# Sums that run on in PSUM: seven-product pairs of a hybrid attention block, and a 16-key tail in one product

## The chip, the cores and the metric

The kernel runs on one core of one Trainium2 chip. The metric is the device time of one execution in microseconds (us), the median of several runs. Before the change it is 909.74 us (three runs, 909.62 to 910.92). Engines are named as in the profile: PE (TensorE, matrix products), DVE (VectorE), ACT (ScalarE), POOL (GpSimd) and SP (SyncE, which here only issues loads).

## The reference

One encoder layer over 16 meta tokens and 1024 tokens of width 1024, everything in float32:

```python
hn = rmsnorm(h, pre_norm_g)
proj = hn @ w_in + b_in          # 1024 -> 5376 columns: q, k, v, z of two branches, gates ga and gb
oa = diff_attention(qa, ka, va)  # dense, 4 heads, two softmaxes each
ob = windowed_gqa(qb, kb, vb)    # each query sees keys within 128, 8 heads on 2 key heads
ya = (oa * silu(za)) @ w_out_a
yb = (ob * silu(zb)) @ w_out_b
mixed = sigmoid(ga) * ya + sigmoid(gb) * yb
h = h + rmsnorm(mixed @ w_out, post_norm_g)
return h[:, 16:]
```

## The kernel before

A float32 operand is held as the sum of a rounded part and a rest ("hi" and "lo", both in the fp32r format that PE multiplies fast), and a product of two operands is three products of parts. ACT (or POOL) rounds, DVE or POOL subtracts: line 791 and 792 in `split`, lines 139 and 140 in `load_w`.

The program is a chain of stages: normalization and transposition of the input, branch B's windowed attention, branch A's dense attention, the gates, the two output projections ("mix"), and the final product with w_out.

**Branch B** goes over four head pairs c and eight query blocks i. `b_trans` transposes the probabilities of a block, `b_values` multiplies them with the values. Block 0 sees two blocks of 128 keys and the 16 meta tokens, and takes the meta tokens as a third block: one matmul with the rounded probabilities and one with their rests.

**The gates** ga and gb (columns 3328 to 5375) and the final product are computed in pairs of 128-column blocks. A pair is one two-by-two block product, and instead of eight block products it takes seven, with sums of operands and of results (Strassen's scheme in Winograd's form). Each of the seven products P1 to P7 is twelve matmuls of 128x512 (line 862) into a PSUM tile of its own (`product`, six tiles). The operands of P1 and P2 and P4 on the weight side are plain; P5, P6, P3 and P7 need weight sums (`total`, line 837, into three "ws" buffers). On the input side P1, P2 and P3 are plain; P4 to P7 need sums of four quarters of the normalized input, which `combos` makes in nine pieces f1, f2, f4, f3 (lines 805 to 823, two pieces each, and a split at the end). Results are combined by DVE, one addition per step (line 871), or copied by ACT (line 869). The results are c11, c12, c21 and c22; a table gives the order of the products and what is added after each. `SEVEN` serves most pairs, `FIRST` the first output pair, `LAST` the last gate pair:

```python
SEVEN = (
    ("P1", (("p1", "P1"),)),
    ("P2", (("c11", "p1", "P2"),)),
    ("P6", (("u2", "p1", "P6"),)),
    ("P5", (("u4", "u2", "P5"),)),
    ("P3", (("c12", "u4", "P3"),)),
    ("P7", (("u3", "u2", "P7"), ("c22", "u3", "P5"))),
    ("P4", (("c21", "u3", "P4"),)))
```

Each ("name", sources) is one ACT copy (one source) or one DVE addition (two). A gate's result goes through a sigmoid (line 766) and, when both halves of a 128-row block are there, ACT stores it (`sg_d`, line 934). An output's result is squared with a row sum (ACT, line 1049), multiplied by the norm's weight (DVE, line 1051), and when a block of 128 rows is complete its inverse norm is computed (`rstd`) and the block is scaled and added to x in two halves (line 1070) and stored.

**Around the first gate pair.** Four products for branch A's z (`gate_a`, lines 884 and 885) run first; in each, the evacuation of the first half calls two pieces of `combos`, so eight pieces are made there and the ninth ahead of P6 of the first gate pair. After each of the four ga pairs `gate_b` loads branch B's z and o, applies silu and multiplies (lines 895 and 896). All these 128x1024 blocks live in the nine slots of one tile TB, handed out in rotation by `tl()`: call n gets slot n modulo 9, and its first writer waits for the last reader of call n - 9.

**What sets the order.** The code names operations in program order, and a scheduler places each on its engine's queue by the time it expects it to be ready; on the chip each engine then goes through its queue in that order. SP issues loads in its own order, and a load whose slot is not free holds up those behind it.

Of the kernel before, what the change touches and what calls it, by code (L numbers as in the profile page):

```python
# [78 lines left out]
def _body(ctx, tc, A, out, dbg, stop):  # L79
# [113 lines left out]
    VBM = sbp.tile([MT, 2, P], F32R, tag="am", name="vbm", bufs=1)  # L193
# [97 lines left out]

    def zeros(*x):
        z = sbp.tile([P, 256], F32, tag="sq", name="zero", bufs=1)[:80]
        pool.memset(z, 0.0)
        for y in x:
            pool.tensor_scalar(y, z[:, :y.shape[1]], 1.0, 1.0, ALU.mult, ALU.mult)
# [75 lines left out]
    def put_b(VB):  # L372
        def put(pt, b0, nb, rows):
            for g in range(2):
                src = pt[:, :, 64 * g:64 * g + 64]
                v = VB[g][:, b0:b0 + nb] if b0 < 8 else VBM[:, g:g + 1]
                hi = v[:, :, :64]
                act.activation(hi, src, AF.Copy)
                dve.tensor_tensor(v[:, :, 64:], src, hi, ALU.subtract)
        return put  # L380
# [39 lines left out]
    def b_trans(i, sb):  # L420
        ah = sbp.tile([P, 4, 256], F32R, tag="ah", name="ah")
        al = sbp.tile([P, 4, 256], F32R, tag="al", name="al")
        if i == 0:
            blocks = ((17, P, 0), (17 + P, P, 1), (1, MT, 8))
        else:
            blocks = tuple((1 + P * j, P, i - 1 + j) for j in range(3 if i < NB - 1 else 2))
        for x in range(0, len(blocks), 2):
            pt = psT.tile([P, 2, 256], F32, tag="pT", name="pT")
            sub = blocks[x:x + 2]
            for y, (o, rows, _) in enumerate(sub):  # L430
                for j in range(2):
                    pe.transpose(out=pt[:rows, y, j * P:(j + 1) * P], in_=sb[:, j, o:o + rows], identity=ident)  # L432
            rows, n = sub[0][1], len(sub)
            act.activation(ah[:rows, x:x + n], pt[:rows, :n], AF.Copy)
            dve.tensor_tensor(al[:rows, x:x + n], pt[:rows, :n], ah[:rows, x:x + n], ALU.subtract)
        return ah, al, blocks

    def b_values(i, ah, al, blocks, g, ob):
        VB = VB_[g]
        pv = psV.tile([P, 512], F32, tag="pv", name="pv")  # L440
        n, last = 0, 2 * len(blocks) - 1
        for a in (ah, al):
            for x, (_, rows, blk) in enumerate(blocks):
# [237 lines left out]
    am = sbp.tile([80, 256], F32R, tag="am", name="am", bufs=1)  # L681
    zeros(am)
# [28 lines left out]
    if stop == "A":  # L711
# [9 lines left out]
    SEVEN = (  # L721
        ("P1", (("p1", "P1"),)),
        ("P2", (("c11", "p1", "P2"),)),
        ("P6", (("u2", "p1", "P6"),)),
        ("P5", (("u4", "u2", "P5"),)),
        ("P3", (("c12", "u4", "P3"),)),
        ("P7", (("u3", "u2", "P7"), ("c22", "u3", "P5"))),
        ("P4", (("c21", "u3", "P4"),)))

    FIRST = (  # L730
        ("P1", (("p1", "P1"),)),
        ("P2", (("c11", "p1", "P2"),)),
        ("P3", ()),
        ("P6", (("u2", "p1", "P6"),)),
        ("P5", (("u4", "u2", "P5"), ("c12", "u4", "P3"))),
        ("P7", (("u3", "u2", "P7"), ("c22", "u3", "P5"))),
        ("P4", (("c21", "u3", "P4"),)))

    LAST = (
        ("P4", ()),  # L740
        ("P6", (("p6", "P6"),)),
        ("P5", (("u4", "p6", "P5"),)),
        ("P7", (("u3", "p6", "P7"), ("u5", "u3", "P5"), ("u6", "u3", "P4"))),
        ("P1", (("p1", "P1"), ("c22", "u5", "P1"), ("c21", "u6", "P1"), ("u7", "u4", "P1"))),
        ("P3", (("c12", "u7", "P3"),)),
        ("P2", (("c11", "p1", "P2"),)))
# [84 lines left out]
    def seven(steps, a, b, room, wroom, result, tmp=None, between={}, cut=None):  # L831

        val = dict(P1=a["a11"], P2=a["a12"], P4=a["a22"])

        def total(n, x, y, op):
            val[n] = wroom.tile([P, 4, P], F32, tag="ws", name="ws", bufs=3)
            dve.tensor_tensor(val[n], x, y, op)  # L837

        def operand(n):
            if n in ("P5", "P6", "P3") and "P5" not in val:  # L840
                total("P5", a["a21"], a["a22"], add)
            if n in ("P6", "P3") and "P6" not in val:
                total("P6", val["P5"], a["a11"], sub)
            if n == "P3":
                total(n, a["a12"], val["P6"], sub)
            if n == "P7":
                total(n, a["a11"], a["a21"], sub)
# [5 lines left out]
        x = {}  # L853
        for n, ops in steps:
            run(between.get(n, ()))
            hi, lo = operand(n)
            for cs in (slice(0, H),) if n != cut else (slice(0, H // 2), slice(H // 2, H)):
                x[n] = product()
                i = 0
                for w, part in ((hi, 0), (hi, 1), (lo, 0)):  # L860
                    for k in range(4):
                        pe.matmul(x[n][:, cs], lhsT=w[:, k], rhs=b[n][part][:, k, cs], start=(i == 0), stop=(i == 11))  # L862
                        i += 1
                for o, *src in ops:
                    if cs.start == 0:
                        x[o] = (tmp and tmp(o)) or room.tile([P, H], F32, tag="c", name="c", bufs=4 if tmp else 6)
                    src = [x[y][:, cs] for y in src]
                    if len(src) == 1:
                        act.activation(x[o][:, cs], src[0], AF.Copy)
                    else:  # L870
                        dve.tensor_tensor(x[o][:, cs], *src, add)  # L871
                    if o[0] == "c":
                        result(o, x[o][:, cs], cs)
            yield

# [24 lines left out]
    for j in range(4):  # L900
# [4 lines left out]
        def evac(ps, st, n, b):  # L905
            if st == QCH[0][0]:
# [4 lines left out]

    def gates(col, m, to, done=None, steps=SEVEN, between={}):

        col += P * m
        v = A["w_in"][0, :, col:col + 2 * P].rearrange("(j k p) c -> j p k c", p=P, j=2)
        a = {}
        for j in range(2):
            r = gp.tile([P, 4, 2 * P], F32, tag="wr4", name="wr4", bufs=3)
            ld(r, v[j])
            for i in range(2):  # L920
                a[f"a{i + 1}{j + 1}"] = r[:, :, i * P:i * P + P]
        count = [0, 0]
# [7 lines left out]
        run(seven(steps, a, IN, gp, gp, result, between=between))  # L930

    for p in range(4):
        s = [tl(), tl()]
        gates(GA, 2 * p, s, lambda c: act.dma_start(sg_d[2 * p + c], s[c]), between={} if p else {"P6": pieces})
        gate_b(p)
    for p in range(4):
        gates(GB, 2 * p, [TB[:, 2 * p + c] for c in range(2)], steps=LAST if p == 3 else SEVEN)
# [86 lines left out]
    with tc.tile_pool(name="fp", bufs=2, side="right", reuse_waits="tile") as fp:  # L1024
# [4 lines left out]
        def out_pair(p):  # L1029
# [9 lines left out]
            def tmp(o):  # L1039
                if o[0] == "c":  # L1040
                    return block(int(o[1]) - 1)[:, H * (int(o[2]) - 1):H * int(o[2])]

            def result(o, v, cs):
# [7 lines left out]
                (pool if last else dve).tensor_tensor(yb[:, c], v, pg[:, c], ALU.mult)  # L1051
# [5 lines left out]
                if last and n[i] in (1, 3):  # L1057
# [22 lines left out]
            return seven(SEVEN if p else FIRST, a, OUT, fp, wsp, result, tmp, cut="P4" if p == 3 else None)  # L1080

        for p in range(4):
            run(out_pair(p))
# [24 lines left out]
```

## Time and profile before

| | us |
|---|---|
| median of three runs | 909.74 (909.62 to 910.92) |
| profiled execution | 907.95 |
| its span | 906.1 |
| PE busy | 858.2 (95%) |
| DVE busy | 680.0 (75%) |
| ACT busy | 488.8 (54%) |
| POOL busy | 380.4 (42%) |

The profile is of one execution, and its own time is 1.79 us under the median. Busy shares are means over very different stages: in the gate and mix stages PE has no pause for 230 us, elsewhere it waits. An engine's timeline gives for each group of equal instructions the start, the duration of the group, the number, and in brackets the idle time before it with what ended it. The granted clock is PE's: 1.00 is 2.4 GHz, 0.50 is 1.2 GHz. Ends of matmuls are modelled, so durations of products are read from start to start.

### The profile page before, as it was taken

How to read it: one execution, taken by the hardware profiler on the slowest of the kernel's cores; microseconds unless marked ns; L12 is line 12 of the kernel's file. 1: busy time of each engine (PE TensorE's matmuls, PEld its weight loads, DVE VectorE, ACT ScalarE, POOL GpSimd, SP SyncE). 2: the span in 40 equal slices, each digit the busy share in tenths (PEclk: the TensorE clock that was granted, in tenths of full speed). 3: DMA queues.
4: the chain of work that ended last, by engine and by line, in shares of the span. 5: the costliest groups of instructions: out<-in, count | busy, mean ns of one | idle time of the engine just before them, and what ended most of it. 6: DMA issues, size and time to landing. Idle time of an engine off the chain costs nothing.

```text
span 906.1 us, 13766 instructions
## 1 busy us (share of the span) xinstructions
PE 858.2 (95%) x4670; PEld 733.9 (81%) x4670; DVE 680.0 (75%) x1432; ACT 488.8 (54%) x975; POOL 380.4 (42%) x482
## 2 busy tenths in 40 slices
PE   4799999999999999999999999399999999999995
PEld 2797988888888898899888887288888888887784
DVE  6735668767988988997877699975444476959897
ACT  4635567766868768877766532344444540114432
POOL 6224543545021212221222189555454555826553
PEclk9999999999999999999999999699999999999998
DMA  8321110215122121021111153464511366311223
GB/s 262 105 50 45 56 57 19 89 43 133 36 71 68 47 72 68 25 71 48 47 65 48 47 185 117 163 210 161 178 56 47 131 231 207 94 63 47 94 95 138
DMA packets 64318, 85.85 MB, mean 95 GB/s; under 512 B 5248, under 2 KB 49294, under 8 KB 64248
## 3 DMA queue, kind: packets, MB, share of 16 engines
q1 hardware_dynamic: 56640, 60.28, 21.1%
q10 hardware_dynamic: 7576, 24.67, 7.9%
q8 instruction: 37, 0.61, 0.3%
q14 instruction: 33, 0.27, 0.1%
q0 software_dynamic: 32, 0.02, 0.0%
HBM read 60.63 MB, written 19.00 MB: 88 GB/s over the span
## 4 chain that ended last, share of the span: by engine, by line
PE 63%; DVE 21%; ACT 7%; issue 5%; POOL 1%; DMA 1%; SPq 0%; DVEq 0%; ACTq 0%; POOLq 0%
PE mm L151 21%; PE pp L862 17%; PE pp L966 9%; PE pv L627 3%; DVE sb L588 3%; PE pv L445 2%; PE pT L432 2%; PE pT L615 2%; PE s L585 2%; DVE sb L598 2%; ACT sb L591 2%; PE s L586 2%; ACT sb L597 1%; DVE ws L837 1%; DVE TB L885 1%
## 5 line engine op out<-in xcount | busy, mean ns | idle before, releaser
L151 PE MATMUL mm<-hn,wh 128*128 128x512 f32 (+2 forms) x896 | 203.6, 356 | 2.9 <-ACT vT L347 1.9
L139 POOL TENSOR_SCALAR wh<-wr 128x256 fp32r<-128x256 f32 x124 | 63.5, 528 | 265.9 <-PE mm L151 237.4
L151 PEld LDWEIGHTS mm<-hn,wh 128*128 128x128 f32 x896 | 145.1, 192 | 19.2 <-ACT vT L347 2.1
L140 POOL TENSOR_TENSOR wl<-wr,wh 128x256 fp32r<-128x256 f32 x124 | 107.4, 890 | 19.4 <-PE mm L151 17.4
L151 PE MATMUL mm<-hn,wl 128*128 128x512 f32 (+2 forms) x448 | 101.5, 353 | 0.0
L792 POOL TENSOR_TENSOR wl<-ws,wh 128x512 fp32r<-128x512 f32 x48 | 71.6, 1501 | 66.0 <-ACT wh L791 52.2
L591 ACT ACTIVATE sb<-sb,st 128x1040 f32<-128x1040 f32 x64 | 74.3, 1162 | 35.2 <-DVE st L588 34.4
L862 PE MATMUL pp<-t,wh 128*128 128x512 f32 (+1 forms) x296 | 73.2, 390 | 15.6 <-ACT wh L791 15.6
L862 PE MATMUL pp<-hn,wh 128*128 128x512 f32 x320 | 79.8, 391 | 0.0
L151 PEld LDWEIGHTS mm<-hn,wl 128*128 128x128 f32 x448 | 73.7, 191 | 7.6
L862 PEld LDWEIGHTS pp<-t,wh 128*128 128x128 f32 x296 | 55.5, 191 | 28.2 <-ACT wh L791 16.9
L588 DVE CUSTOM_DVE_ANT_0 sb<-s,U,st 128x346 f32<-128x346 f32 x128 | 73.1, 574 | 5.8
L871 DVE TENSOR_TENSOR c<-c,pp 128x512 f32<-128x512 f32 x70 | 47.4, 682 | 38.5 <-PE pp L862 36.7
L862 PEld LDWEIGHTS pp<-hn,wh 128*128 128x128 f32 x320 | 60.1, 188 | 13.2
L585 PE MATMUL s<-K,Q 128*128 128x346 f32 (+1 forms) x192 | 65.8, 345 | 0.9 <-DVE st L588 0.4
L586 PE MATMUL s<-K,Q 128*128 128x346 f32 (+1 forms) x192 | 61.3, 321 | 0.0
L598 DVE SCALAR_TENSOR_TENSOR sb<-sb,st 128x1040 f32<-128x1040 f32 x32 | 43.9, 1372 | 13.2 <-ACT sb L597 12.9
L413 ACT ACTIVATE sb<-sb,st 128x385 f32<-128x385 f32 (+2 forms) x64 | 37.5, 588 | 22.6 <-DVE st L410 20.3
L417 POOL TENSOR_SCALAR sb<-sb,st 128x384 f32<-128x384 f32 (+2 forms) x64 | 35.5, 568 | 32.5 <-DVE st L415 32.4
L791 ACT ACTIVATE wh<-ws 128x512 fp32r<-128x512 f32 x48 | 29.7, 625 | 35.0 <-PE pp L862 20.1
L410 DVE CUSTOM_DVE_ANT_0 sb<-s,TB,nsink 128x384 f32<-128x384 f32 (+2 forms) x64 | 35.4, 580 | 16.6 <-PE s L408 15.0
L617 DVE TENSOR_TENSOR al<-pT,ah 128x512 fp32r<-128x512 f32 x64 | 43.7, 686 | 3.6 <-ACT ah L616 2.9
(212 smaller groups left out, 1928.7 us busy)
## 6 DMA issues: line engine op xcount, KB each, us to landing
wr<-in_w_in_dram SPq DMA_DIRECT2D x96, 128.0 KB, 2.5
wr<-in_w_in_dram SPq DMA_DIRECT2D x16, 512.0 KB, 3.6
K<-K ACTq DMA_DIRECT2D x16, 260.0 KB, 3.5
xt<-in_x_dram SPq DMA_DIRECT2D x8, 512.0 KB, 7.1
sg_d<-TB ACTq DMA_DIRECT2D x8, 512.0 KB, 2.6
w<-in_w_out_dram SPq DMA_DIRECT2D x4, 1024.0 KB, 5.5
room<-sg_d SPq DMA_DIRECT2D x8, 512.0 KB, 4.8
fx<-in_x_dram SPq DMA_DIRECT2D x8, 512.0 KB, 4.6
```

What stands on the lines that cost most here:

```text
L139: pool.tensor_scalar(hi, raw, 1.0, 1.0, ALU.mult, ALU.mult)
L140: pool.tensor_tensor(lo, raw, hi, ALU.subtract)
L151: pe.matmul(ps[:, :n], lhsT=w[k // 4][:, k % 4, :], rhs=hslice(part, k, st, n), start=(i == 0), stop=(i == 3 * KC - 1))
L585: pe.matmul(s, lhsT=q, rhs=KH[:, m, o:o + n], start=True, stop=False)
L586: pe.matmul(s, lhsT=q, rhs=KL[:, m, o:o + n], start=False, stop=True)
L588: dve.tensor_tensor_reduce(out=sb[:, o:o + n], in0=s, in1=back(U, u0 + o, n), scale=-0.125, scalar=lim, op0=ALU.add, op1=ALU.min, accum_ou ...
L591: act.activation(sb, sb, AF.Exp, bias=st[:, m:m + 1], scale=-1.0, accum_out=st[:, 2 + m:3 + m])
L598: dve.scalar_tensor_tensor(sbs[0], sbs[0], st[:, 4:5], sbs[1], ALU.mult, ALU.add)
L792: lo_eng.tensor_tensor(t[1][:, k], x, t[0][:, k], sub)
L862: pe.matmul(x[n][:, cs], lhsT=w[:, k], rhs=b[n][part][:, k, cs], start=(i == 0), stop=(i == 11))
L871: dve.tensor_tensor(x[o][:, cs], *src, add)
L966: pe.matmul(py, lhsT=w[:, k, :], rhs=g[h][:, k], start=(i == 0), stop=(i == 11))
```

## The change

1. `seven` and its tables become a class `Pair` with three orders: `first` (first gate pair and first output pair), `plain` (most pairs), `last` (last gate pair).
2. In `plain`, P6 and P7 and P4 are accumulated into the PSUM tile of P1 (X), and P3 into that of P5 (Z). ACT copies X after P1 and after P6, and Z after P5; DVE makes three additions instead of seven; c21 is read from PSUM by its consumer.
3. In `last`, P7 goes into P6's tile, P3 into P5's and P2 into P1's.
4. The first gate pair takes the order of `first`, P3 in third place. The pieces f3 and the final split of `combos` are called after P3, no longer in the fourth z product.
5. At the last output block the product with the norm's weight goes to POOL only for the right half, and the two scalings of the other block are called at the second and third result instead of the first and third.
6. Branch B's block 0 takes the meta tokens in one product: rounded values and their copy in rows 0 to 15 and 64 to 79 of an 80-row tile (VBM), rounded probabilities and rests in the same rows of `am`, zeros between.

```diff
-    VBM = sbp.tile([MT, 2, P], F32R, tag="am", name="vbm", bufs=1)
+    VBM = sbp.tile([80, 2, P], F32R, tag="sh", name="vbm", bufs=1)
...
+    am = sbp.tile([80, 256], F32R, tag="am", name="am", bufs=1)
...
-        zeros(*vm)
+        zeros(*vm, VBM, am)
...
-            blocks = ((17, P, 0), (17 + P, P, 1), (1, MT, 8))
+            blocks = ((17, P, 0), (17 + P, P, 1))
...
+            act.activation(am[:MT], pt[:MT, 0], AF.Copy)
+            dve.tensor_tensor(am[64:80], pt[:MT, 0], am[:MT], ALU.subtract)
...
+        if i == 0:
+            pe.matmul(pv[:, :256], lhsT=VBM[:, g, :], rhs=am, start=False, stop=True)
...
+        def mul(self, n, ps=None, cuts=(slice(0, H),), done=None):
+
+            old = ps is not None
+            if not old:
+                ps = product()
+            hi, lo = self.operand(n)
...
+                        pe.matmul(ps[:, cs], lhsT=w[:, k], rhs=self.b[n][part][:, k, cs], start=(i == 0 and not old),
+                                  stop=(i == 11), skip_group_check=True)
...
+                if done:
+                    self.out(done, ps[:, cs], cs)
...
+        def plain(self, cuts=(slice(0, H),)):
+            X = self.mul("P1")
+            p1 = self.copy(X)
+            self.sum(p1, self.mul("P2"), "c11")
+            yield
+            self.mul("P6", X)
+            u2 = self.copy(X)
+            yield
+            Z = self.mul("P5")
+            p5 = self.copy(Z)
+            self.mul("P7", X)
+            self.sum(p5, X, "c22")
+            yield
+            self.mul("P3", Z)
+            self.sum(u2, Z, "c12")
+            yield
+            self.mul("P4", X, cuts, "c21")
+            yield
...
+        def first(self, between=lambda: None):
+            p1 = self.copy(self.mul("P1"))
+            self.sum(p1, self.mul("P2"), "c11")
+            p3 = self.mul("P3")
+            between()
+            u2 = self.sum(p1, self.mul("P6"))
+            p5 = self.mul("P5")
+            u4 = self.sum(u2, p5)
+            self.sum(u4, p3, "c12")
+            u3 = self.sum(u2, self.mul("P7"))
+            self.sum(u3, p5, "c22")
+            self.sum(u3, self.mul("P4"), "c21")
...
+        def last(self):
+            V = self.mul("P4")
+            X = self.mul("P6")
+            p6 = self.copy(X)
+            Z = self.mul("P5")
+            p5 = self.copy(Z)
+            self.mul("P7", X)
+            x = self.copy(X)
+            Y = self.mul("P1")
+            u = self.sum(x, Y)
+            self.sum(u, V, "c21")
+            self.sum(u, p5, "c22")
+            w = self.sum(p6, Y)
+            self.mul("P3", Z)
+            self.sum(w, Z, "c12")
+            self.mul("P2", Y, done="c11")
...
-            if st == QCH[0][0]:
+            if st == QCH[0][0] and j < 3:
                 next(pieces)
                 next(pieces)
...
     for p in range(4):
         s = [tl(), tl()]
-        gates(GA, 2 * p, s, lambda c: act.dma_start(sg_d[2 * p + c], s[c]), between={} if p else {"P6": pieces})
+        x = gate(GA + 2 * P * p, s, lambda c: act.dma_start(sg_d[2 * p + c], s[c]))
+        if p:
+            run(x.plain())
+        else:
+            x.first(lambda: run(pieces))
         gate_b(p)
...
-                (pool if last else dve).tensor_tensor(yb[:, c], v, pg[:, c], ALU.mult)
+                (pool if last and t else dve).tensor_tensor(yb[:, c], v, pg[:, c], ALU.mult)
...
-                if last and n[i] in (1, 3):
+                if last and n[i] > 1:
                     rest.pop(0)()
```

How it moves instructions, at three places.

DVE around the first gate pair. L821 to L823 (L804 to L806 after the change) are the two last pieces f3, L837 (L829) the weight sums, L884 and L885 (L937, L938) the gate products of branch A's z. Before:

```order
L821 TENSOR_TENSOR TB<-hn_87 128x1024 x2
L822 TENSOR_TENSOR TB<-TB,hn_89 128x1024 x2
L823 TENSOR_TENSOR TB<-TB,hn_89 128x1024 x2
L884 SCALAR_TENSOR_TENSOR c<-pp,binT,c 128x512
L837 TENSOR_TENSOR ws<-wr_6649,wr_6651 128x512
L885 TENSOR_TENSOR TB<-c,TB 128x512
L884 SCALAR_TENSOR_TENSOR c<-pp,binT,c 128x512
L837 TENSOR_TENSOR ws<-ws,wr_6649 128x512
L885 TENSOR_TENSOR TB<-c,TB 128x512
L837 TENSOR_TENSOR ws<-wr_6651,ws 128x512
```

After the change:

```order
L829 TENSOR_TENSOR ws<-wr_6642,wr_6644 128x512
L804 TENSOR_TENSOR TB<-hn_87 128x1024
L829 TENSOR_TENSOR ws<-ws,wr_6642 128x512
L805 TENSOR_TENSOR TB<-TB,hn_89 128x1024
L937 SCALAR_TENSOR_TENSOR c<-pp,binT,c 128x512
L829 TENSOR_TENSOR ws<-wr_6644,ws 128x512
L938 TENSOR_TENSOR TB<-c,TB 128x512
L806 TENSOR_TENSOR TB<-TB,hn_89 128x1024
L804 TENSOR_TENSOR TB<-hn_87 128x1024
L829 TENSOR_TENSOR ws<-wr_6642 128x512
```

The three weight sums of P5, P6 and P3 (the first three ws rows) were behind both pieces f3, and now stand among them; the second piece begins behind them.

SP in the gate stage. TB<-zb_d and TB<-ob_d load z and o for `gate_b` (pairs 0 to 3), wr_6812 and wr_6814 (before), wr_6811 and wr_6813 (after) are the two weight quarters of gate pair 1, the next two those of pair 2. Before:

```order
L116 DMA TB<-ob_d 128x1024
L116 DMA TB<-zb_d 128x1024 x2
L116 DMA TB<-ob_d 128x1024 x2
L116 DMA wr_6814<-in_w_in_dram 128x4x256
L116 DMA TB<-zb_d 128x1024
L116 DMA wr_6971<-in_w_in_dram 128x4x256
L116 DMA wr_6973<-in_w_in_dram 128x4x256
L116 DMA TB<-ob_d 128x1024
L116 DMA TB<-zb_d 128x1024
```

After the change:

```order
L116 DMA TB<-ob_d 128x1024
L116 DMA TB<-zb_d 128x1024
L116 DMA wr_6813<-in_w_in_dram 128x4x256
L116 DMA TB<-ob_d 128x1024
L116 DMA TB<-zb_d 128x1024
L116 DMA wr_6962<-in_w_in_dram 128x4x256
L116 DMA wr_6964<-in_w_in_dram 128x4x256
L116 DMA TB<-zb_d 128x1024
L116 DMA TB<-ob_d 128x1024 x2
```

Before, the loads of z for pairs 0 and 1 stand next to each other at the top. After the change the second zb_d row is that of pair 2, whose slot comes free earlier; z of pair 1 is the third zb_d row and o of pair 1 the row behind it, after both weight quarters of pair 2.

ACT from output pair 0 to pair 1. junk<-fy are the squares of c22 and c21 of pair 0, out_dram<-fy the store of its first block, c<-pp the copy of P1 of pair 1. Before:

```order
L1049 ACTIVATE junk,fs<-fy 128x512
L791 ACTIVATE wh<-ws 128x512
L1074 DMA out_dram<-fy 128x1024
L1049 ACTIVATE junk,fs<-fy 128x512
L869 ACTIVATE c<-pp 128x512
L791 ACTIVATE wh<-ws 128x512
L161 ACTIVATE fs<-fs,eps_76 128x1
```

After the change:

```order
L1112 ACTIVATE junk,fs<-fy 128x512
L774 ACTIVATE wh<-ws 128x512
L1137 DMA out_dram<-fy 128x1024
L1112 ACTIVATE junk,fs<-fy 128x512
L868 ACTIVATE c<-pp 128x512
L774 ACTIVATE wh<-ws 128x512
L161 ACTIVATE fs<-fs,eps_76 128x1
```

The order is the same: the copy of P1 of pair 1 stands behind the store and the square of c21. What differs is who reads on: the next product into that tile, P6, is the third of pair 1.

## Rows read from the trace of the kernel before

**Rows 1.** Page, part 1: busy us, share of the span, instructions of each engine.

```profile
PE 858.2 (95%) x4670; PEld 733.9 (81%) x4670; DVE 680.0 (75%) x1432; ACT 488.8 (54%) x975; POOL 380.4 (42%) x482
```

**Rows 2.** Busy by stretch: start:end, length, PE, PEld, DVE, ACT, POOL, clock, DMA, GB/s.

```profile
600.00:650.00 50.00, 50.00 (x221) 41.13 (x220) 29.41 (x37) 22.34 (x35) 26.61 (x19) 1.00 0.52 179
...
570.00:575.00 5.00, 0.00 (x0) 0.00 (x0) 5.00 (x5) 2.87 (x4) 1.74 (x1) 0.52 0.35 105
...
584.00:585.00 1.00, 1.00 (x6) 0.83 (x5) 1.00 (x1) 0.00 (x0) 1.00 (x2) 1.00 0.45 66
```

**Rows 3.** Timeline of PE: start, us, engine, line, operation, count, idle before and releaser.

```profile
580.89 3.45 PE L862 MATMUL pp<-t,wh 128*128 128x512 f32 x8 [14.69 <-ACT wh L791]
...
590.56 1.98 PE L862 MATMUL pp<-hn,wh 128*128 128x512 f32 x8
...
604.30 1.98 PE L862 MATMUL pp<-t,wh 128*128 128x512 f32 x8
...
607.02 1.98 PE L862 MATMUL pp<-hn,wh 128*128 128x512 f32 x8
```

**Rows 4.** Timeline of DVE, first gate pair.

```profile
566.29 2.35 DVE L821 TENSOR_TENSOR TB<-hn 128x1024 f32<-128x1024 f32 x2
...
573.76 2.41 DVE L837 TENSOR_TENSOR ws<-wr,wr 128x512 f32<-128x512 f32 x1
...
580.70 0.68 DVE L837 TENSOR_TENSOR ws<-wr,ws 128x512 f32<-128x512 f32 x1
...
590.13 1.71 DVE L837 TENSOR_TENSOR ws<-wr,wr 128x512 f32<-128x512 f32 x1 [1.95 <-DMA wr<-in_w_in_dram]
...
594.68 2.06 DVE L871 TENSOR_TENSOR c<-c,pp 128x512 f32<-128x512 f32 x3
```

**Rows 5.** Timeline of PE, output stage.

```profile
842.61 1.98 PE L862 MATMUL pp<-t,wh 128*128 128x512 f32 x8
...
848.76 2.12 PE L862 MATMUL pp<-t,wh 128*128 128x512 f32 x8 [0.55 <-ACT wh L791]
...
873.91 2.12 PE L862 MATMUL pp<-t,wh 128*128 128x512 f32 x8 [0.35 <-ACT wh L791]
...
895.50 0.64 PE L862 MATMUL pp<-t,wl 128*128 128x256 f32 x4
```

**Rows 6.** Timeline of POOL, first gate pair.

```profile
573.26 5.10 POOL L792 TENSOR_TENSOR hn<-TB,hn 128x1024 fp32r<-128x1024 f32 x2 [7.45 <-ACT hn L791]
...
588.71 4.30 POOL L792 TENSOR_TENSOR wl<-wr,wh 128x512 fp32r<-128x512 f32 x3
```

**Rows 7.** Timeline of SP, which issues the loads.

```profile
569.07 6.90 SPq L116 DMA_DIRECT2D TB<-zb_d  x2
```

**Rows 8.** DMA issues: queue, operation, count, KB each, median us to landing.

```profile
sg_d<-TB ACTq DMA_DIRECT2D x8, 512.0 KB, 2.6
...
TB<-zb_d SPq DMA_DIRECT2D x4, 512.0 KB, 3.4
```

**Rows 9.** Timeline of ACT, gate stage.

```profile
598.78 1.06 ACT L766 ACTIVATE TB<-TB 128x1024 f32<-128x1024 f32 x1 [0.44 <-DMA sg_d<-TB]
...
601.03 0.72 ACT L766 ACTIVATE TB<-c,binT 128x512 f32<-128x512 f32 x1 [1.19 <-DVE c L871]
```

**Rows 10.** Timeline of ACT, output pairs 0 and 1.

```profile
846.99 0.63 ACT L1049 ACTIVATE junk<-fy 128x512 f32<-128x512 f32 x1 [4.27 <-DVE fy L871]
...
847.62 0.58 ACT L869 ACTIVATE c<-pp 128x512 f32<-128x512 f32 x1
```

**Rows 11.** Timeline of DVE, output pairs 0 and 1.

```profile
843.23 2.46 DVE L1070 SCALAR_TENSOR_TENSOR fy<-fy,fs,fx 128x512 f32<-128x512 f32 x2
...
846.22 0.67 DVE L871 TENSOR_TENSOR fy<-c,pp 128x512 f32<-128x512 f32 x1
```

**Rows 12.** Timeline of DVE, end of the program.

```profile
897.61 1.79 DVE L1070 SCALAR_TENSOR_TENSOR fy<-fy,fs,fx 128x512 f32<-128x512 f32 x1
...
901.63 1.41 DVE L1070 SCALAR_TENSOR_TENSOR fy<-fy,fs,fx 128x512 f32<-128x512 f32 x2
```

More of the change, by code (lines that the diff above doesn't have):

```diff
@@ L712, in _body @@
         return
[L721 to L746, printed above, removed]
     H = T // 2
@@ L851, in operand @@
             return hi, lo
[L853 to L858, printed above, removed]
+        def mul(self, n, ps=None, cuts=(slice(0, H),), done=None):
[3 more added lines that the diff above has]
+            hi, lo = self.operand(n)
+            for cs in cuts:
                 i = 0
@@ L874, in seven, with new, copy, sum @@
-            yield
+                if done:
+                    self.out(done, ps[:, cs], cs)
+            return ps
+        def new(self, name=None):
+            return (name and self.tmp and self.tmp(name)) or self.room.tile([P, H], F32, tag="c", name="c", bufs=self.bufs)
+        def copy(self, ps):
+            x = self.new()
+            act.activation(x, ps, AF.Copy)
+            return x
+        def sum(self, x, ps, name=None):
+            y = self.new(name)
+            dve.tensor_tensor(y, x, ps, add)
+            if name:
+                self.out(name, y, slice(0, H))
+            return y
@@ L921, in gates, with gate @@
                 a[f"a{i + 1}{j + 1}"] = r[:, :, i * P:i * P + P]
+        return a
+    def gate(col, to, done=None):
         count = [0, 0]
@@ L929, in result @@
                 done(c)
-        run(seven(steps, a, IN, gp, gp, result, between=between))
+        return Pair(IN, gp, gp, result, quarters(col))
     for p in range(4):
         s = [tl(), tl()]
-        gates(GA, 2 * p, s, lambda c: act.dma_start(sg_d[2 * p + c], s[c]), between={} if p else {"P6": pieces})
+        x = gate(GA + 2 * P * p, s, lambda c: act.dma_start(sg_d[2 * p + c], s[c]))
[3 more added lines that the diff above has]
+            x.first(lambda: run(pieces))
         gate_b(p)
     for p in range(4):
-        gates(GB, 2 * p, [TB[:, 2 * p + c] for c in range(2)], steps=LAST if p == 3 else SEVEN)
+        x = gate(GB + 2 * P * p, [TB[:, 2 * p + c] for c in range(2)])
+        if p < 3:
+            run(x.plain())
+        else:
+            x.last()
     cG.close()
@@ L1079, in result @@
                         half(t)
-            return seven(SEVEN if p else FIRST, a, OUT, fp, wsp, result, tmp, cut="P4" if p == 3 else None)
+            pair = Pair(OUT, fp, wsp, result, a, tmp, bufs=4)
+            if p:
+                run(pair.plain((slice(0, H // 2), slice(H // 2, H)) if p == 3 else (slice(0, H),)))
+            else:
+                pair.first()
         for p in range(4):
-            run(out_pair(p))
+            out_pair(p)
 _INS = ['x', 'meta_tokens', 'rel_bias', 'pre_norm_g', 'w_in', 'b_in', 'lambda_q1', 'lambda_k1', 'lambda_q2',
```

69 lines of the change are left out of this document (33 added, 36 removed).

## The prediction

> **What bounds the kernel now.** I read the busy totals first: TensorE works 858.2 us of a span of 906.1 [rows 1]. Time can be won only where it stands still, and a new standstill goes straight to the end. The table by stretch says where it never does: from 600 to 650 us, in the gate stage, it is busy for all 50.00 us [rows 2], so fewer VectorE additions there buy nothing. The timeline of TensorE shows the holes. The large one is in the first gate pair: P6 starts only at 580.89, after 14.69 us of idleness, so P2 ended at 566.20 [rows 3]. The granted clock is near half from 570 on and at full speed again from 584 [rows 2]; so P6's first eight matmuls take 3.45 us where those of another product take 1.98 [rows 3]. VectorE is late there: from 566.29 it works without a hole through the last input sum, the gate products and the weight sums [rows 4]. It is a backlog, not one late instruction. In the output stage there are two small holes, of 0.55 and 0.35 us, and behind the last matmul, which ends at 896.14 (895.50 + 0.64) [rows 5], a tail of 10 us.
>
> The sum is made against the profiled execution: 907.95 us, that is its span of 906.1 and 1.85 around it. It lies 1.79 below the median of 909.74, and I put the same difference on the median. A measurement here can tell about 0.2% (1.8 us) from no change.
>
> **The change part by part.** A product is twelve matmuls and takes 2.72 us (604.30 to 607.02 [rows 3]).
>
> *First gate pair, the input sum.* P3 needs no input sum, only three weight sums. In the new VectorE order these stand between pieces of the input sum: three of 0.68, two pieces of 1.18 (2.35 for two [rows 4]) and a gate product of 0.7 bring P3's operand to about 571.4, and after ScalarE's rounding of 0.6 TensorE starts near 572 instead of 580.89. P3, P6 and P5 are done at 581.5, slow clock included. But P7 needs the last piece of the input sum. VectorE now does it behind P7's weight sum, and that one waits for a buffer until GpSimd has split P5's weights. GpSimd starts at 571.8 and has three weight splits of 1.43 and one input split of 2.55 to do [rows 6]: 6.8 us, and up to 1.8 more where VectorE's sums come between. So VectorE, ready at 576.2, goes on between 578.6 and 580.4. I get 584.5 for the last piece, 588 for its split and 591 for P7's end, against 593.28 (590.56 + 2.72 [rows 3]): 2.5 us won here.
>
> *What becomes of it.* The sum for block c12 is the 23rd VectorE instruction from 566.29 in both orders, with the same kinds before it: six for the input sum, four gate products, seven weight sums, two for gate B, three results. Another order among them cannot make it earlier. It ended near 595.3 (first of the three at 594.68 [rows 4]); on the way VectorE had waited 1.95 us for weights [rows 4], and now it waits 2.4 to 4.2 for that buffer. I take 595.3, with 593.3 and 597.5 as bounds. And c12 now has a successor in TensorE's path. The room for z of gate_b(1) used to be free when an input sum had been split, near 576 (573.26 + 2.55 [rows 6]), and SP loaded it then, as the second z of [rows 7]. With the pieces moved, the count of tl() gives that z the room of the first gate result, and SP can load it only after the result is stored. The chain from c12: sigmoid 0.72, rounding 0.6, store 2.6, load 3.4, sigmoid of z 1.06, product 1.18, c11 0.68, its sigmoid 0.72, rounding 0.6, copy of P1+P6 0.58, and 0.5 for handovers: 12.6 us ([rows 4, 8, 9, 10]; roundings like the copy). These stand ahead of the copy in ScalarE's order, and P7 of pair 1, which now runs on in that bank, waits for it: 595.3 + 12.6 = 607.9. Before, the product in that fifth place started at 607.02 [rows 3]. So **the hole is mostly filled and the gain is lost: +0.9**. Bounds: -3 (TensorE reaches pair 1 that much earlier, and z is no longer late) and +3.1 (c12 at 597.5).
>
> The Trainium skill, in SBUF — State Buffer, Who interferes with whom, states that a VectorE instruction with two SBUF inputs and a GpSimd instruction that reads SBUF shut each other out, the second waiting for the whole of the first. The 2.41 us of a weight sum that takes 0.68 alone [rows 4] bear it out; by that rule, taken for every sum behind 572, c12 comes at its late bound and the front costs 3.1.
>
> *Later gate pairs.* Each has four VectorE additions fewer and two ScalarE copies more; TensorE's full 50 us cover both. A copy has one product (2.72 us) before its bank is written again, and at most a rounding and a sigmoid (1.3) stand before it: nothing. If the weights came late, that cover would be gone and each copy's 0.58 would count. In the last gate pair four additions of 0.69 [rows 4] must have read the bank within 2.72 us: +0.3, bounds 0 and +1.5.
>
> *Branch B.* Four matmuls fewer, one per head pair; at the mean of 0.184 us (858.2 / 4670 [rows 1]) that is 0.7: -0.5, bounds 0 and -0.74. The zeroing on GpSimd moves ahead, beside the first projections: nothing.
>
> *Output stage, pair 1.* Here the change adds a wait. P6 of pair 1 runs on in the bank of P1, so it needs ScalarE's copy of P1. Before, nobody needed that copy soon: ScalarE made it at 847.62 [rows 10], behind the square of c21 of pair 0, which waits for VectorE; VectorE does two scalings of together 2.46 and a product first and sums c21 at 846.22 [rows 11]. P6 meanwhile ran from 842.61 [rows 5]. ScalarE's new order is the same at this place: store of a finished block, square of c21, copy. VectorE has one weight sum less before it (0.6), so the copy ends at 847.6 instead of 848.2, and P6 starts then: 847.6 - 842.6 = **+5.0**, bounds 4.4 and 5.6. The large hole brought the clock down [rows 2], so I add a slow restart, 3.45 - 1.98 = 1.4 (bounds 0 and 1.5). The holes of 0.55 and 0.35 before P3 [rows 5] close, since the fifth place is now P7's, whose weight sum is made a pair ahead; with twice 0.14 of slower restart that is -1.2 (0 to -1.2). In pairs 2 and 3 the copy of P1+P6 stands behind the square of c11, with about a microsecond to spare: +0.3 (0 to +3).
>
> *Tail.* From 896.14 to the last two scalings at 901.63 [rows 12] are 5.5 us. c21 is now read from PSUM, without its last addition of 0.4, and the scaling of 1.79 [rows 12] no longer meets GpSimd's product (0.7 alone): -1.5, bounds 0 and -2.5.
>
> Sum: 0.9 + 0.3 - 0.5 + 5.0 + 1.4 - 1.2 + 0.3 - 1.5 = **+4.7**. On the profiled 907.95 that is 912.65, on the median **914.4 us**.
>
> **The rivals.**
> (a) *The hole's gain survives*: z is loaded early enough and pair 1 starts 3 us earlier; the rest as above. For it: by my own walk P7 ends 2.5 earlier. Against it: VectorE's unchanged amount of work and z's new room. Time: 914.4 - 3.9 = 910.5, no change.
> (b) *Faster*: the copy of P1 in output pair 1 is not late, nor those behind it. It decides whether c21 of pair 0 is summed by 841.2, so that square and copy (0.63 and 0.58 [rows 10]) are over by 842.6. For it: VectorE has less to do in this stage. Against it: only 0.6 of that lies before c21. Then 6.4 and 0.3 are not lost: 907.7, and with (a) 903.8.
> (c) *VectorE and GpSimd shut each other out*, in the front (c12 at 597.5, 2.2 more) and in the output pairs, whose copies are each a microsecond late (2 more): 918.6. The weight sum of 2.41 speaks for it, and it is the Trainium skill's rule named above; against it, c12 kept its time among such sums before.
> (d) *TensorE doesn't run on in the bank*: the order shows P6 of output pair 1 waiting on ScalarE and fewer additions, so I give it no chance of its own.
>
> **How the numbers follow.** Forecast 0.52 (mostly 911.6 to 917), (a) 0.22, (b) 0.11, (c) 0.15. Slower by over 0.2% (above 911.6): the forecast, (c), and 0.09 of (a) where the output costs more: 0.76. Within 0.2%: 0.13 of (a) and 0.01 of (b): 0.14. Faster (below 907.9): the rest of (b), 0.10. The range leaves out (b) and the far end of (c): 909.0 to 918.2.
>
> **What would show it.** Right: P3's matmuls near 572, and a new wait of TensorE on ScalarE's copy, of 0 to 3 us, at the fifth product of gate pair 1; in the output stage a hole of 5 us before the third product of pair 1, ended by the copy, at half clock after it, and nothing like it in pairs 2 and 3; the last scalings 4 us behind the last matmul. Wrong: TensorE going from 572 to the output stage in one piece with pair 1 at 593, or no hole at that third product.

## The result and the profile after

The changed kernel takes 915.75 us (median of four, 914.18 to 917.12), the kernel before 909.99 us (four, 909.62 to 910.92). The ratio is 1.0063, with a 95% interval of 1.0044 to 1.0081: slower by 5.7 us. The forecast was 914.4. The profiled execution of after is its slowest (917.12, span 915.3), and that of before (907.95, span 906.1) is faster than all four of its runs, so the two traces differ by 9.2 us of span and the medians by 5.8; differences between the traces are read here only place by place.

Page of after, part 1:

```profile
PE 862.0 (94%) x4666; PEld 735.1 (80%) x4666; DVE 651.0 (71%) x1395; ACT 499.3 (55%) x996; POOL 379.8 (41%) x480
```

VectorE lost 29 us of work against [rows 1], and the kernel is slower: the work that it lost had not been on TensorE's path.

TensorE's timeline of after shows its holes (stretches in which it stands idle) of over 0.5 us from the first gate pair on (start, duration, line, operation, count, idle before and what ended it):

```profile
570.92 3.78 PE L856 MATMUL pp<-hn,wh 128*128 128x512 f32 x8 [5.71 <-ACT wh L774]
...
583.81 1.65 PE L856 MATMUL pp<-hn,wh 128*128 128x512 f32 x6 [2.09 <-ACT wh L774]
...
588.00 1.20 PE L856 MATMUL pp<-hn,wl 128*128 128x512 f32 x4 [1.50 <-POOL wl L775]
...
598.37 2.11 PE L856 MATMUL pp<-t,wh 128*128 128x512 f32 x8 [0.84 <-ACT c L868]
...
606.57 3.69 PE L856 MATMUL pp<-hn,wh 128*128 128x512 f32 x8 [2.48 <-ACT c L868]
...
731.11 2.12 PE L856 MATMUL pp<-hn,wh 128*128 128x512 f32 x8 [1.89 <-DVE c L873]
...
751.74 1.65 PE L1030 MATMUL pp<-t,wh 128*128 128x512 f32 x6 [1.02 <-POOL wh L139]
...
852.54 3.61 PE L856 MATMUL pp<-t,wh 128*128 128x512 f32 x8 [5.05 <-ACT c L868]
...
879.37 2.11 PE L856 MATMUL pp<-o,wh 128*128 128x512 f32 x8 [0.51 <-ACT c L868]
...
906.89 1.22 PE L856 MATMUL pp<-t,wh 128*128 128x256 f32 x8 [1.30 <-DVE fs L162]
```

The hole of 14.69 of [rows 3] has shrunk to 5.71 and the small ones behind it. In its place stand waits that before has nowhere from there on. All with "c L868" are for ScalarE's copy of a product whose tile is to be written again. The one with "c L873" is for VectorE's sum in the last gate pair. In the last row the second half of P4 waits, as I read it, until the readers of the first half of the same tile are done: VectorE's product with the norm's weight, the later of the two, ends at 906.84 and the matmuls start at 906.89; the profile names fs L162, which ends at 906.89. In outs_apart and no_run_on (below), where each half has a tile of its own, this wait is absent. The holes of [rows 5] are gone. The table by stretch (start:end, length, PE, PEld, DVE, ACT, POOL, granted clock, DMA, GB/s) shows what follows the two longest waits: eight matmuls in 3.69 and 3.61 us, at half clock.

```profile
604.00:606.50 2.50, 0.10 (x1) 0.00 (x0) 1.93 (x4) 1.70 (x3) 1.69 (x2) 1.00 0.47 157
606.60:610.00 3.40, 3.40 (x8) 2.72 (x9) 0.56 (x1) 1.12 (x2) 2.96 (x2) 0.50 0.57 196
...
852.60:856.00 3.40, 3.40 (x9) 2.67 (x10) 3.14 (x6) 1.23 (x3) 2.56 (x2) 0.53 0.43 171
```

Why the copy is late in output pair 1 stands in the timelines of ScalarE and VectorE (after), the places of [rows 10, 11]:

```profile
850.02 0.36 ACTq L1137 DMA_DIRECT2D out_dram<-fy  x1
851.29 0.63 ACT L1112 ACTIVATE junk<-fy 128x512 f32<-128x512 f32 x1 [4.10 <-DVE fy L873]
...
851.91 0.58 ACT L868 ACTIVATE c<-pp 128x512 f32<-128x512 f32 x1
```

```profile
848.58 1.42 DVE L1133 SCALAR_TENSOR_TENSOR fy<-fy,fs,fx 128x512 f32<-128x512 f32 x2
...
850.51 0.68 DVE L873 TENSOR_TENSOR fy<-c,pp 128x512 f32<-128x512 f32 x1
...
910.80 1.41 DVE L1133 SCALAR_TENSOR_TENSOR fy<-fy,fs,fx 128x512 f32<-128x512 f32 x2
```

The copy stands behind two things in ScalarE's queue: the store of a finished block, issued when VectorE's scalings end (848.58 + 1.42 = 850.0), and the square of c21, which waits for the sum at 850.51. TensorE had ended that c21's product at 841.90, so VectorE's sum starts 8.6 us behind it. The Trainium skill (PSUM — Partial Sum Buffer, Engine vs sequencer instructions) says that ScalarE's queue is strictly first in, first out; the trace agrees: P1, started at 841.90 and 2.72 us long, was complete some 7 us before the copy began.

### The profile page after: what moved, and what is told of

It reads as the page before. It is cut to its first block, busy times and chain, and to the rows that moved or that the text cites. A ratio compares the mean times of both kernels' runs of the same rounds, so it can differ in the third digit from the quotient of the medians.

```text
span 915.3 us, 13664 instructions
## 1 busy us (share of the span) xinstructions
PE 862.0 (94%) x4666; PEld 735.1 (80%) x4666; DVE 651.0 (71%) x1395; ACT 499.3 (55%) x996; POOL 379.8 (41%) x480
## 4 chain that ended last, share of the span: by engine, by line
PE 58%; DVE 17%; ACT 7%; issue 6%; POOL 6%; DMA 4%; SPq 0%; DVEq 0%; ACTq 0%; POOLq 0%
PE mm L151 20%; PE pp L856 16%; PE pp L1030 7%; DVE sb L599 3%; PE pv L638 2%; PE s L596 2%; PE pT L436 2%; PE s L597 2%; DVE ws L829 2%; DMA wr<-in_w_out_b_dram 2%; PE pT L626 2%; PE pv L454 2%; DVE sb L609 2%; POOL wl L140 2%; ACT sb L602 2%
## 5 line engine op out<-in xcount | busy, mean ns | idle before, releaser
L856 PE MATMUL pp<-hn,wh 128*128 128x512 f32 x320 | 83.8, 405 | 12.5 <-ACT wh L774 7.8
L873 DVE TENSOR_TENSOR c<-c,pp 128x512 f32<-128x512 f32 x32 | 21.7, 684 | 42.3 <-PE pp L856 41.9
L775 POOL TENSOR_TENSOR wl<-wr,wh 128x512 fp32r<-128x512 f32 x24 | 35.8, 1500 | 25.3 <-PE pp L856 14.1
```

The lines of the kernel that those rows point to most:

```text
L775: lo_eng.tensor_tensor(t[1][:, k], x, t[0][:, k], sub)
L856: pe.matmul(ps[:, cs], lhsT=w[:, k], rhs=self.b[n][part][:, k, cs], start=(i == 0 and not old), stop=(i == 11), skip_group_check=True)
```

## The experiments

Each ratio is to runs of the kernel before on the same chip. Their medians are 910.04 (first four experiments), 909.85 (the next four: outs_apart, gate1_apart, no_run_on, branch_b) and 908.98 (late_run_on, out3_run_on, old_tail). The ratio of the changed kernel, 1.0063 (1.0044 to 1.0081), is what to compare with.

**Undoing output pair 1 alone.** In `out_pair`, with a method that has the products and additions of `SEVEN`, each product in its own tile:

```diff
-            if p:
+            if p == 1:
+                run(pair.apart())
+            elif p:
```

> Output pair 1 alone gets its seven products back in separate PSUM tiles, with the additions of before; all else as in the changed kernel (915.75 us). Theory (the wait for ScalarE's copy of P1 is the cost of the output stage): the hole of 5.05 us before its third product and the half clock after it (1.6) go, and at most 1.2 of small holes before P3 comes back: -5.5 to -6.7, so 909 to 910.3. Rival (VectorE is behind in this stage, and the copy is only where it shows): the additions come back on VectorE and the hole turns up at a later product: under 2 us gained, 914 or more.

Measured: 915.58 us, ratio 1.0061 (1.0045 to 1.0076): nothing won. TensorE's timeline:

```profile
871.11 3.78 PE L856 MATMUL pp<-t,wh 128*128 128x512 f32 x8 [4.10 <-ACT c L868]
```

Pair 1 has only its old hole of 0.66, and the wait for a copy, with the half clock, stands a pair later, at P6 of pair 2. My theory of one badly placed copy fell. The rival (the lateness is VectorE's, and shows wherever the next copy is needed) forecast both the hole at a later product and the time.

**The copy ahead of the square.** c21 of pair 0 is squared, and its block normed, only behind the next pair's first copy:

```diff
...
             p1 = self.copy(X)
+            while held:
+                with tc.issue_after(self.copied.ins):
+                    held.pop()()
...
```

> The square of c21 of output pair 0, and the norm of its block, are queued on ScalarE behind the copy of P1 of pair 1. Theory as the prediction had it (the copy waits behind that square): the copy comes some 5 us earlier and 6 us are won, 909.5 to 911. Rival, read from the trace of after: the store of the finished block stands ahead of the copy as well, and ScalarE issues it only when VectorE's scalings are done, at 850.02; then the copy ends near 851.6 instead of 852.5, and 0 to 1.2 us are won, 914.5 to 916.

Measured: 915.17 us, 1.0056 (1.0043 to 1.0069). The hole is 4.16 us instead of 5.05: the 0.9 us that the rival forecast. The time cannot be told from that of the changed kernel. The prediction had named the square and not the store.

**Square and store out of the way.** As above, and

```diff
-                        act.dma_start(out[0, b * P:(b + 1) * P, :], yb)
+                        sp.dma_start(out[0, b * P:(b + 1) * P, :], yb)
```

> As square_behind, and the stores of whole output blocks are issued by SyncE instead of ScalarE. Theory (ScalarE goes through its queue in order, and store and square together held the copy): now only roundings stand ahead of the copy, it ends near 848, P6 of pair 1 starts about 1 us behind P2's end instead of 5.05, and the clock does not fall: 4 to 5.6 us less than the changed kernel, 910 to 911.8. Rival (the copy is late for another reason, or SyncE's waiting stores hold up the loads of x behind them): under 2 us gained, or a new wait for fx.

Measured: 917.40 us, 1.0079 (1.0061 to 1.0096): nothing won. TensorE and, in the second fence, ScalarE:

```profile
847.66 2.11 PE L858 MATMUL pp<-t,wh 128*128 128x512 f32 x8 [0.77 <-ACT c L870]
...
858.55 3.78 PE L858 MATMUL pp<-o,wh 128*128 128x512 f32 x8 [5.16 <-ACT c L870]
```

```profile
851.73 0.63 ACT L1119 ACTIVATE junk<-fy 128x512 f32<-128x512 f32 x1 [4.12 <-DVE fy L875]
...
855.60 0.29 ACT L161 ACTIVATE fs<-fs,eps 128x1 f32<-128x1 f32 x1 [2.63 <-DVE fs L1126]
856.77 0.63 ACT L1119 ACTIVATE junk<-fy 128x512 f32<-128x512 f32 x1 [0.88 <-DVE fy L875]
```

The first copy is freed as expected (hole 0.77). Then the second copy, of P1+P6, which P7 needs, stands behind the same late squares, and the 5 us are paid there. So the step was right about the queue and wrong about the cause: in this stage ScalarE's queue is full of work that waits for VectorE, and VectorE is late. It sums c21 of pair 0 at 850.96 here, 9.7 us after TensorE ended that product (841.29). The rival's other half, that stores in SyncE's queue hold up the loads of x, did not come: no wait of VectorE for such a load stands in this trace from 835 us on.

**A free slot for z of gate pair 1.**

```diff
-                x = tl().rearrange("p (k t) -> p k t", k=2)
+                x = (f3s.pop(0) if f3s else tl()).rearrange("p (k t) -> p k t", k=2)
...
-    pieces = combos()
+    pieces, f3s = combos(), []
...
+    f3s += [tl(), tl()]
     for p in range(4):
         s = [tl(), tl()]
```

> The last two input pieces take their slots of TB ahead of the first gate results, as before the change, so z of the second gate pair finds a free slot. Theory (late load, late sigmoid and the queues behind it held the copy in gate pair 1): the wait of 2.48 us before the fifth product of pair 1 goes, and with it the half clock after it (1.7): 3.5 to 4.3 us less, 911.4 to 912.3. Rival 1: the clock fell for what was before that wait, then only 2.5 us less, 913.2. Rival 2 (VectorE's backlog holds the copy anyway): under 0.5 us, 915.2 or more.

Measured: 918.37 us, 1.0090 (1.0077 to 1.0103), by the ratios 2.5 us slower than the changed kernel, with intervals that just overlap. TensorE and ScalarE:

```profile
600.59 2.85 PE L856 MATMUL pp<-t,wh 128*128 128x512 f32 x8 [2.35 <-ACT c L868]
```

```profile
597.87 1.06 ACT L749 ACTIVATE TB<-TB 128x1024 f32<-128x1024 f32 x1 [2.02 <-DMA sg_d<-TB]
```

The sigmoid of z no longer waits for z's load. It has moved ahead of the copy of P1, and waits for its output slot until the first gate result is stored. The hole of 2.48 before P7 is gone and one of 2.35 before P6 has come. From the start of P2 in the first gate pair to the start of gate pair 2 TensorE takes 54.5 us; in the traces with the gates of after it is 52.5 to 54.2. So nothing is won and the copy is late anyway, as in rival 2. The rest of the loss lies in the last gate pair (a hole of 2.31 and a slow restart of 3.46); why there is not settled.

**All output pairs apart; gate pair 1 apart.** In the first, `pair.plain(` becomes `pair.apart(` for pairs 1 to 3; in the second, of the gates:

```diff
-            run(x.plain())
+            run(x.apart() if p == 1 else x.plain())
```

> All output pairs get separate PSUM tiles and the additions of before; gates as in the changed kernel (915.75 us). Theory (running on needs each copy within one product, and ScalarE's queue, held by VectorE's backlog, does not give it; one pair undone only moved the hole to the next): the hole of 5.05 and its half clock of 1.6, the 0.51 in pair 2 and the 1.30 in the last product go, up to 1.2 of small holes comes back: -6.0 to -8.5, 907.3 to 909.8. Rival (this stage is bound by VectorE's work, which grows by four additions a pair): a hole remains somewhere, 913 or more.

> Gate pair 1 alone gets separate PSUM tiles and its additions back. Theory (there the waits of 0.84 and 2.48 and the half clock of 1.7 are the price of running on, and VectorE has room in the gate stage to catch up in that pair): -3.5 to -5.0, 910.8 to 912.3. Rival (the backlog of the first gate pair is handed on, as in the output stage): the same hole shows in gate pair 2, 0 to -1, 914.8 to 915.8.

Measured: outs_apart 912.84 us, 1.0030 (1.0018 to 1.0042); gate1_apart 918.65 us, 1.0104 (1.0087 to 1.0121). TensorE of gate1_apart:

```profile
621.75 3.67 PE L856 MATMUL pp<-t,wh 128*128 128x512 f32 x8 [4.06 <-ACT c L868]
```

With pair 1 undone, gate pair 2 pays 4.06 us and a half clock: more than pair 1 had. The rival had the place right; the time, by the ratios 3.7 us slower than the changed kernel, lies outside both forecasts. What holds ScalarE there (gate1_apart) is not a sum of VectorE:

```profile
619.03 1.06 ACT L749 ACTIVATE TB<-TB 128x1024 f32<-128x1024 f32 x1 [4.06 <-DMA sg_d<-TB]
```

The sigmoid of z stands ahead of the copy and waits for a slot of TB until the store of a gate result has landed, 6.2 us after its issue at 612.77, where the median of such stores is 2.6. In outs_apart the output stage has no wait for a copy left. Its last product starts at 896.9 where that of after starts at 904.0; but from there to the end of the span it takes 13.7 us against 11.3, so a third of the 7.1 us is lost in the tail. By the ratios 3.0 us are won; with these 2.4 it would be 5.4, still short of the 6.0 forecast. The tail is the larger part of the miss, and the rest is not settled.

**Running on nowhere.** The order of the first gate pair, branch B's single product and the new calls at the last block stay; every product has its own tile (`apart`, and the table `LAST` for the last gate pair).

> No sum runs on in PSUM anywhere; kept are the new order of the first gate pair, branch B's meta tokens in one product, and the new order at the last output block. Theory (the reordered front is a gain of 2 to 4 us in itself, which only the waits for copies took back): against the kernel before, -1.0 from branch B, -2 to -3.2 from the front, 0 to -1 from the tail: 904.8 to 907. Rival (VectorE's amount of work up to c12 sets the time of pair 1 in any order): only branch B and the tail, 908 to 909.

Measured: 905.07 us, 0.9949 (0.9937 to 0.9961): **faster than both kernels**, by 4.6 us against before and, by the two ratios (1.0063 / 0.9949), by some 10 us against the change. The theory held, and its rival (c12's time sets pair 1 in any order, 908 to 909) fell.

This trace also tells what running on costs, before it is paid. The copies of P1 in gate pairs 1 to 4 and output pairs 1 to 3, where nobody waits for them (ScalarE, no_run_on):

```profile
601.21 0.60 ACT L868 ACTIVATE c<-pp 128x512 f32<-128x512 f32 x1 [0.40 <-ACT TB L749]
...
621.52 0.60 ACT L868 ACTIVATE c<-pp 128x512 f32<-128x512 f32 x1 [0.40 <-PE pp L856]
...
637.12 0.60 ACT L868 ACTIVATE c<-pp 128x512 f32<-128x512 f32 x1 [0.40 <-PE pp L856]
...
654.26 0.60 ACT L868 ACTIVATE c<-pp 128x512 f32<-128x512 f32 x1 [1.34 <-PE pp L856]
...
845.41 0.58 ACT L868 ACTIVATE c<-pp 128x512 f32<-128x512 f32 x1
...
863.90 0.58 ACT L868 ACTIVATE c<-pp 128x512 f32<-128x512 f32 x1
...
882.03 0.58 ACT L868 ACTIVATE c<-pp 128x512 f32<-128x512 f32 x1
```

and the starts of P6 in the same pairs (TensorE, no_run_on), which here write a tile of their own:

```profile
599.28 1.99 PE L856 MATMUL pp<-t,wh 128*128 128x512 f32 x8
...
618.47 1.99 PE L856 MATMUL pp<-t,wh 128*128 128x512 f32 x8
...
637.66 1.99 PE L856 MATMUL pp<-t,wh 128*128 128x512 f32 x8
...
656.84 1.99 PE L856 MATMUL pp<-t,wh 128*128 128x512 f32 x8
...
840.29 1.98 PE L856 MATMUL pp<-t,wh 128*128 128x512 f32 x8
...
860.31 1.98 PE L856 MATMUL pp<-t,wh 128*128 128x512 f32 x8
...
880.00 1.98 PE L856 MATMUL pp<-t,wh 128*128 128x512 f32 x8
```

The end of the copy less the start of P6 is the hole to come if that pair is the first to run on. A negative number means that the copy is early:

| pair | read from no_run_on | measured, and in which kernel |
|---|---|---|
| gate 1 | 601.81 - 599.28 = 2.5 | 2.35 in z_slot; 0.84, then 2.48 at P7, in after; none, then 1.97 and 1.94 at P7, in square_behind and outs_apart |
| gate 2 | 622.12 - 618.47 = 3.7 | 4.06 in gate1_apart |
| gate 3 | 637.72 - 637.66 = 0.1 | not tried as the first |
| gate 4 | 654.86 - 656.84 = -2.0 | none in late_run_on (below) |
| output 1 | 845.99 - 840.29 = 5.7 | 5.05 in after |
| output 2 | 864.48 - 860.31 = 4.2 | 4.10 in out1_apart |
| output 3 | 882.61 - 880.00 = 2.6 | 2.48 in out3_run_on (below) |

The rows on gate 4 and output 3 were written down before their kernels ran. Four of the six places come within 0.7 us of the reading and gate 4 shows no wait, as read; at gate 1 the reading, taken from another kernel, fits z_slot alone.

**Running on where the copies are early, and where they are late.** no_run_on with `plain` for the three gate pairs 4 to 6; and with `plain` for the last output pair:

```diff
-                run(pair.apart((slice(0, H // 2), slice(H // 2, H)) if p == 3 else (slice(0, H),)))
+                run((pair.plain if p == 3 else pair.apart)((slice(0, H // 2), slice(H // 2, H)) if p == 3 else (slice(0, H),)))
```

> As no_run_on (905.07 us), but the fifth to seventh gate pair run on in PSUM, as in the changed kernel. Theory (the price of running on is the lateness of ScalarE's copy of P1 behind the end of P2, and it can be read beforehand: in the trace of no_run_on the copies of gate pairs 1 to 4 end 2.5, 3.7 and 0.1 us after P2's end and then 2 us before it): no wait of TensorE on a copy there, and neither gain nor loss, 904.5 to 905.7. Rival 1 (the first pair that runs on pays, wherever it stands): a hole of about 4 us in the fifth pair, 909 or more. Rival 2 (twelve VectorE additions fewer are worth something): 904 or less.

> As no_run_on, but the last output pair runs on in PSUM. Theory: its copy of P1 ends at 882.6 in the trace of no_run_on, 2.6 us after P2's end, so P6 starts after a hole of 2.2 to 3.0, the last product gets its 1.3 us wait between its halves, and the tail is 1.5 to 2.4 shorter: 905.07 + 2.6 + 1.3 - 2.0 = 907, between 906 and 908.5 (a slow clock after the hole included). Rival (each pair can pay with what it saves): no hole, only the shorter tail, 903 to 904.5.

Measured: late_run_on 905.47 us, 0.9960 (0.9948 to 0.9972); out3_run_on 907.43 us, 0.9982 (0.9972 to 0.9991). Holes of TensorE in the last output pair of out3_run_on, and the clock behind the first of them:

```profile
881.77 2.11 PE L856 MATMUL pp<-t,wh 128*128 128x512 f32 x8 [2.48 <-ACT c L868]
...
888.86 2.12 PE L856 MATMUL pp<-o,wh 128*128 128x512 f32 x8 [1.35 <-ACT c L868]
...
897.34 1.21 PE L856 MATMUL pp<-t,wh 128*128 128x256 f32 x8 [1.30 <-DVE fs L162]
```

```profile
881.80:885.00 3.20, 3.20 (x14) 2.67 (x15) 2.89 (x6) 0.82 (x2) 2.25 (x2) 1.00 0.37 150
```

Both as read. In late_run_on P6 of the fifth pair starts at 655.68 without a wait (the last fence of this part), and twelve additions fewer on VectorE win nothing that the two intervals could show. In out3_run_on the hole came within 0.2 us of the reading; the 1.35 before P7 (the second copy) had not been in it. TensorE, late_run_on:

```profile
652.90 2.01 PE L856 MATMUL pp<-hn,wh 128*128 128x512 f32 x8
...
655.68 1.99 PE L856 MATMUL pp<-t,wh 128*128 128x512 f32 x8
```

**The old tail, and branch B alone.** no_run_on with the old calls at the last block (`pool if last`, `n[i] in (1, 3)`); and the kernel before with point 6 of the change alone.

> As no_run_on, but both halves of the last block's product with the norm's weight are GpSimd's again and the two scalings are called at the first and third result, as before the change. Theory (from the start of the last product to the end of the span no_run_on takes 13.7 us and the kernel before 13.0; the new order helps only where c21 is read from PSUM): -0.4 to -0.8, 904.3 to 904.7. Rival: no difference, 904.9 to 905.3.

> The kernel before with branch B's meta tokens in one product, and nothing else changed. Theory (the trace of after starts the first gate pair 0.99 us earlier): -0.7 to -1.0, 909.0 to 909.3. Rival 1, the term of the prediction: -0.5. Rival 2 (the four matmuls are hidden, and the 0.99 is the scatter of two executions): within 0.3 of the kernel before.

Measured: old_tail 904.85 us, 0.9953 (0.9940 to 0.9966), which these runs cannot tell from no_run_on. branch_b 908.37 us, 0.9984 (0.9976 to 0.9993): 0.6 to 2.2 us faster, 1.5 in the middle. That covers the theory (0.7 to 1.0) and excludes both rivals (0.5, and within 0.3).

## Why the prediction was right, and where it was not

Sign and size came out, and the wait that it named as the main cost is there: P6 of output pair 1 on the copy of P1, 5.05 us for a forecast of 5.0, with a slow restart of 3.61 - 1.98 = 1.6 for 1.4 (the forecast's own 3.45 - 1.98 is 1.47). That the sum of 4.7 came so near to the 5.8 measured is in part luck: the last gate pair and the mix stage cost 1.89 and 1.02 us for 0.3 and nothing, and branch B gave 1.5 for 0.5. Point by point:

- *First gate pair.* P3 starts at 570.92 ("near 572"). P7 ends at 589.03, 4.2 us earlier than before; of this 1.0 had been won ahead of the pair (its P2 starts at 562.26, before at 563.25). VectorE waited 1.18 us for the buffer of P7's weight sum, not 2.4 to 4.2. c12 came 1.3 us earlier than taken, and 1.0 of that is the same lead: its sigmoid starts at 594.07. From 594.0 to the end of the copy are 12.5 us; the chain of the forecast, of which the fence below shows the last links (ScalarE, after), had 12.6, and P7 starts at 606.57 for 607.9. Not foreseen were the 0.84 before P6 and, after a pause of only 2.48, the half clock, 3.69 - 1.98 = 1.7 us. These two are not in every trace of these gates: in square_behind and outs_apart, whose gates are those of after, the first pair ends 1.5 to 1.7 us later, counted from its P2; P6 of the next does not wait, and P7 comes at full clock (the first two fences below). From the start of P2 in the first pair to the start of gate pair 2 TensorE takes 54.2 us in after, 52.7 and 52.5 in these two, 51.9 in before and 53.0 in branch_b, whose gates are those of before. So "the hole is mostly filled and the gain is lost" holds, and for its +0.9 the traces give anything from -0.5 to +2.3.
- *The shutting out of VectorE and GpSimd.* By the Trainium skill's rule (SBUF — State Buffer, Who interferes with whom), as the prediction applied it, c12 would have come at 597.5. Weight sums of 0.7 us do take 1.6 to 1.8 there (586 to 592 in after), but c12 came 3.5 us before that bound.
- *What becomes of it.* The step "z's new room makes the load late, and the copy behind it" describes the trace of after, but taking the late load away (z_slot) won nothing: the time was lost at P6. The copies of gate pairs 1 and 2 are late (2.5 and 3.7 us in no_run_on) even with the tiles apart, behind sigmoids that wait for whatever comes last there: a sum of VectorE (3.26 us, gate 1) or the store of a gate result (3.74 us, gate 2).
- *The gain of the front* ("2.5 us won here") is real. no_run_on beats branch_b by 0.0035, 3.2 us, with the front as the main difference. Rival (a) was right about its own half.
- *Output stage.* The number was right, the reason too narrow: "behind the square of c21" is one of at least three waits on VectorE in that queue, and removing square and store moved the hole to P7.
- *Pairs 2 and 3*: 0.51 for 0.3.
- *Branch B*: 0.6 to 2.2 won for a term of 0.5 with a bound of 0.74. Four matmuls at the mean row do not give the 1.5 in the middle; what else was saved is open.
- *Last gate pair*: the term of 0.3 (bounds 0 and 1.5) was too small. TensorE waited 1.89 for VectorE's sum. Four additions of 0.69 had to read the tile or stand before the last that did, as foreseen; not foreseen was that VectorE began them only at 728.46, behind six splits for the mix stage, when P1 had ended at 726.11.
- *Mix stage*: 1.02 lost on weights that GpSimd rounds; their load had come late (GpSimd waited 9.69 us for it, to 747.32). The wait stands in after, out1_apart (0.76) and late_run_on (0.40), not in gate1_apart or outs_apart. Not predicted, not settled.
- *Tail.* From the start of the last product to the end of the span 11.3 us for 13.0 before: 1.7 for a forecast of 1.5. The agreement is two errors: the wait of 1.30 between its halves was not foreseen, and behind the last matmul more was won than forecast. The last scalings start 2.2 us behind its end (910.80 after 908.58), where 4 had been named and before has 5.5.

TensorE in gate pair 1, a row of square_behind and one of outs_apart:

```profile
605.95 2.11 PE L858 MATMUL pp<-hn,wh 128*128 128x512 f32 x8 [1.97 <-ACT c L870]
```

```profile
606.42 2.11 PE L856 MATMUL pp<-hn,wh 128*128 128x512 f32 x8 [1.94 <-ACT c L868]
```

ScalarE in gate pair 1 (after):

```profile
601.85 1.06 ACT L749 ACTIVATE TB<-TB 128x1024 f32<-128x1024 f32 x1 [3.01 <-DMA TB<-zb_d]
...
604.80 0.72 ACT L749 ACTIVATE TB<-c,binT 128x512 f32<-128x512 f32 x1 [1.37 <-DVE c L873]
...
605.95 0.57 ACT L868 ACTIVATE c<-pp 128x512 f32<-128x512 f32 x1
```

The sigmoid of z waits 3.01 us for its load, the sigmoid of c11 for the sum behind the gate product, and the copy goes last.

## What to carry to other kernels

Accumulating on into a PSUM tile turns an evacuation that nobody waited for into one that the next matmul waits for. Before doing it, read in the trace how late the evacuation ends behind the matmul that would need it: that lateness is about the price, it is paid at the first tile that runs on or the next, and a half clock can come on top. Moving single instructions in the queue, or undoing one pair, only moved the place here. Additions taken from an engine that is not the bottleneck won nothing, not even twelve of them.

## What had not been expected of the hardware

The pause after which TensorE came back at half clock was shorter than the traces of before had shown (14.69 us of idleness there): 3.69 us for eight matmuls after 2.48 us, granted clock 0.50. It is not fixed by the pause alone: after 2.48 us in out3_run_on they took 2.11 at full clock (1.00), after 1.97 in square_behind 2.11 at 1.00, and after 2.35 in z_slot 2.85 (0.70). What else decides it is not shown here.
